# Grouped-query attention with two-bank score tiles, and the softmax's scale moved into the queries

## The chip, the core and the metric

The kernel runs on one core of one Trainium2 chip. A core has five engines that this text names: PE (TensorE, matrix multiplication, with its weight loads shown as PEld), DVE (VectorE), ACT (ScalarE), POOL (GpSimd) and SP (SyncE, which issues the DMAs here). Matmuls write to PSUM, which has 8 banks of 512 fp32 columns for each of 128 partitions; DVE and ACT read them from there. The metric is the device time of one execution in microseconds (us), lower is better.

## The reference

The program is a two-layer diffusion block on 512 image tokens and 256 context tokens with 1024 features, in fp32. Layer 0 has a feed-forward part, grouped-query attention and a second feed-forward part; layer 1 has differential attention in the attention's place. The change is in grouped-query attention alone: 16 query heads share 4 key and value heads of 64 columns. Cut to what matters:

```python
def sink_softmax(s):
    m = jnp.maximum(jnp.max(s, axis=-1, keepdims=True), sink)
    e = jnp.exp(s - m)
    return e / (jnp.sum(e, axis=-1, keepdims=True) + jnp.exp(sink - m))

# image queries, in blocks of 128: keys within 128 positions, and all context keys
s_loc = where(mask, einsum('bqkgd,bskd->bkgqs', qb, kb) * scale, NEG_INF)
s_ctx = einsum('bqkgd,bckd->bkgqc', qb, kc) * scale          # scale = 64 ** -0.5 = 0.125
p = sink_softmax(concatenate([s_loc, s_ctx], axis=-1))
out = einsum(p[..., :span], vb) + einsum(p[..., span:], vc)
# context queries attend to the context keys alone
```

## The kernel before

Activations lie transposed, features on partitions and the 768 tokens along the columns. To hold fp32 accuracy on a faster format, each operand is split into a high and a low part (`w_hi` and `w_lo`, `xh` and `xl`, `kh` and `kl`, `pth` and `ptl`), and a product is two or three matmuls. `weights` (L54 to L56) loads a weight block by DMA, ACT rounds it to the high part, POOL subtracts for the low part.

The function `gqa` is one stage of the program. Its PSUM is divided into pools: `pgqa` (1 bank, `half`) for the projections, `pgqa_t` (2 banks, `tr`) for transposes, `pgqa_v` (1 bank, `av`) for the weighted values and `pgqa_s` (4 banks, `s`) for scores. A tile of a pool is given out again when its last reader is done, in a ring.

The stage first projects one unit of keys, two of queries and one of values, through the score banks, in two halves of 384 tokens each (`project_halves`, L285; the second half has two more columns, which become the unit's bias, L289). `norm_halves` sums the squares of the input with a matmul of ones (L248) and computes the inverse root into `rstd` on ACT and DVE (`rsqrt`, L218 to L223); `scaled_halves` (L297) multiplies the projections by it. `rope` (L319 to L327) rotates queries and keys.

Then 24 steps follow, 4 key heads with 6 blocks of 128 queries each. A step computes the scores of four heads against 512, 640, 640, 512, 256 and 256 keys (`scores`). Each head has a bank of its own, or two where the keys are 640 (384 and 256 columns). Per bank: two matmuls (L437, L438), for image blocks one or two that add the mask (L441), a maximum on DVE (L443), the exponential on ACT with its sum (L450). For 640 keys the two maxima are merged (L446). L447 multiplies the maximum by -0.125 and takes the minimum with the negated sink. L453 to L457 make the reciprocal of the sum for four heads at once, and L460 (DVE) and L463 (POOL) scale the probabilities. `values` transposes them (L475), splits them (L478 on ACT, L479 on DVE), multiplies by the values (L480, L481) and puts the heads together (L485 to L494).

The loop issues the scores of step i+1, then a projection of a later unit or a part of the output projection (L520) as filling work, then the values of step i. The order on each engine is not written by hand: a scheduler fixes it at build time from its own estimate of durations, and each engine then works strictly in that order, waiting on semaphores.

## Time and profile before

| | |
|---|---|
| three runs | 2901.63, 2899.31, 2900.96 us, median 2900.96 |
| the profiled execution | 2902.44 us, of which its span 2900.6 us |
| mean granted TensorE clock | 0.982 |

The profile's stretches, in us busy of each engine:

| stretch (us) | what runs | PE | DVE | ACT | POOL | clock |
|---|---|---|---|---|---|---|
| 0 to 630 | start, feed-forward | 585.5 | 389.6 | 165.2 | 265.6 | 0.97 |
| 630 to 1000 | grouped-query attention | 336.7 | 284.3 | 213.6 | 169.4 | 0.96 |
| 1000 to 1900 | feed-forward, twice | 894.2 | 398.4 | 211.6 | 350.3 | 1.00 |
| 1900 to 2400 | differential attention | 476.3 | 298.6 | 208.1 | 257.1 | 0.99 |
| 2400 to 2900 | rest, feed-forward | 477.4 | 185.0 | 173.9 | 268.8 | 0.99 |

Matmuls are pipelined and their ends are modelled, so PE counts as busy also where it is not at its peak. An idle time is named by the instruction that waited and the one that ended the wait; where the wait had several conditions, by the last. In a group's row stand the line, the engine, the operation, output and inputs, shapes, the count, then the busy time in us and the mean duration in ns, then the idle time before them.

### The profile page before, as it was taken

The numbers are of one execution on the slowest core, as the hardware profiler recorded it, in microseconds if no ns is written. First come the engines' busy times: TensorE is split into PE (matmuls) and PEld (weight loads), VectorE is DVE, ScalarE is ACT, GpSimd is POOL, SyncE is SP. The second block draws the span as 40 slices with busy tenths as digits, with TensorE's granted clock in tenths as the row PEclk, the third lists the DMA queues.
The fourth block names the chain that finished last, engine by engine and source line by source line (L and its number), as shares of the span: only waits on it lengthen the run. The fifth ranks groups of instructions, "written<-read, shape, count | busy, mean of one in ns | idle before, by whom it ended". The sixth has DMA issues, their size and how long they took to land. (4 is left out here: it accounts for less than half of the span.)

```text
span 2900.6 us, 40961 instructions
## 1 busy us (share of the span) xinstructions
PE 2770.0 (95%) x16150; PEld 2593.4 (89%) x16150; DVE 1555.9 (54%) x2683; ACT 972.4 (34%) x1749; POOL 1311.2 (45%) x762
## 2 busy tenths in 40 slices
PE   5899999999989899999999999999989999999998
PEld 3899999989877799999998999999988887799998
DVE  7955555567887544444447333344467678522223
ACT  4322122145666421221224212221345555422223
POOL 4443343355443443333335433333465665555553
PEclk7999999999999999999999999999999999999999
DMA  6333333333242323233223232232232333233331
GB/s 240 121 112 108 125 105 118 124 115 100 82 144 81 99 78 112 76 106 117 74 90 106 75 118 84 91 120 88 85 98 74 90 89 114 83 92 100 102 105 44
DMA packets 113423, 296.38 MB, mean 102 GB/s; under 512 B 12880, under 2 KB 30928, under 8 KB 113232
## 3 DMA queue, kind: packets, MB, share of 16 engines
q1 hardware_dynamic: 112944, 293.66, 31.8%
q8 instruction: 128, 2.10, 0.3%
q14 instruction: 63, 0.52, 0.1%
q10 hardware_dynamic: 288, 0.10, 0.0%
HBM read 260.42 MB, written 15.20 MB: 95 GB/s over the span
## 5 line engine op out<-in xcount | busy, mean ns | idle before, releaser
L56 POOL TENSOR_TENSOR w_lo<-w_raw,w_hi 128x1024 fp32r<-128x1024 f32 (+2 forms) x377 | 802.1, 2128 | 1072.1 <-ACT w_hi L55 1055.6
L266 PE MATMUL big<-xh,w_hi 128*128 128x384 f32 (+3 forms) x2816 | 696.6, 328 | 38.7 <-DVE xh L831 19.5
L55 ACT CAST w_hi<-w_raw 128x1024 fp32r<-128x1024 f32 (+2 forms) x377 | 337.4, 895 | 1132.6 <-PE big L70 394.1
L266 PE MATMUL big<-xl,w_hi 128*128 128x384 f32 (+3 forms) x2816 | 693.6, 327 | 8.3 <-DVE xl L832 5.0
L266 PE MATMUL big<-xh,w_lo 128*128 128x384 f32 (+3 forms) x2816 | 693.6, 328 | 2.3 <-POOL w_lo L56 2.3
L266 PEld LDWEIGHTS big<-xh,w_hi 128*128 128x128 f32 x2816 | 502.5, 191 | 47.2 <-DVE xh L831 22.3
L266 PEld LDWEIGHTS big<-xl,w_hi 128*128 128x128 f32 x2816 | 500.3, 191 | 10.5 <-DVE xl L832 6.3
L266 PEld LDWEIGHTS big<-xh,w_lo 128*128 128x128 f32 x2816 | 497.8, 190 | 3.8 <-POOL w_lo L56 3.3
L131 DVE SCALAR_TENSOR_TENSOR ada_junk<-w_raw,s_bc 128x1024 f32<-128x1024 f32 x224 | 342.4, 1546 | 291.6 <-DMA w_raw<-ada_w 290.4
L271 DVE COPY bias<-big 128x2 f32<-128x2 f32 x176 | 27.7, 157 | 621.1 <-PE big L266 620.9
L68 PE MATMUL big<-hh,w_hi 128*128 128x512 f32 (+1 forms) x1200 | 327.6, 344 | 0.0
L70 PE MATMUL big<-hl,w_hi 128*128 128x512 f32 (+1 forms) x1200 | 327.3, 344 | 0.0
L72 PE MATMUL big<-hh,w_lo 128*128 128x512 f32 (+1 forms) x1200 | 326.8, 344 | 0.0
L311 DVE SCALAR_TENSOR_TENSOR hT<-big,mod,hT 128x512 f32<-128x512 f32 (+1 forms) x288 | 167.6, 618 | 176.7 <-PE big L72 176.4
L70 PEld LDWEIGHTS big<-hl,w_hi 128*128 128x128 f32 x1200 | 226.1, 188 | 29.5
L72 PEld LDWEIGHTS big<-hh,w_lo 128*128 128x128 f32 x1200 | 225.0, 188 | 28.6
L68 PEld LDWEIGHTS big<-hh,w_hi 128*128 128x128 f32 x1200 | 224.9, 188 | 27.2
L966 POOL TENSOR_TENSOR hl<-tb,hh 128x768 fp32r<-128x768 f32 (+1 forms) x88 | 152.3, 1730 | 183.2 <-ACT hh L965 181.9
L961 DVE SCALAR_TENSOR_TENSOR tb<-tb,bias,ta 128x512 f32<-128x512 f32 (+1 forms) x154 | 176.1, 1177 | 8.7 <-DVE tb L304 0.5
L285 PE MATMUL half<-xh,w_hi 128*128 128x384 f32 (+3 forms) x464 | 155.5, 335 | 20.6 <-DVE ta L297 18.8
L965 ACT CAST hh<-tb 128x768 fp32r<-128x768 f32 (+1 forms) x88 | 68.7, 781 | 276.5 <-DVE tb L961 276.5
L285 PE MATMUL half<-xl,w_hi 128*128 128x384 f32 (+3 forms) x464 | 153.8, 331 | 0.0
(215 smaller groups left out, 3677.6 us busy)
## 6 DMA issues: line engine op xcount, KB each, us to landing
w_raw<-ffn_gu SPq DMA_DIRECT2D x176, 512.0 KB, 3.3
w_raw<-ada_w SPq DMA_DIRECT2D x128, 512.0 KB, 3.3
w_raw<-ffn_d SPq DMA_DIRECT2D x96, 256.0 KB, 2.7
w_raw<-ffn_d SPq DMA_DIRECT2D x64, 320.0 KB, 2.9
w_raw<-diff_in SPq DMA_DIRECT2D x24, 512.0 KB, 3.2
ada_raw<-ada_w SPq DMA_DIRECT2D x16, 512.0 KB, 7.2
w_raw<-gqa_in SPq DMA_DIRECT2D x12, 512.0 KB, 3.5
og<-god SPq DMA_DIRECT2D x6, 768.0 KB, 6.5
```

The lines of the kernel that those rows point to most:

```text
L55: nc.scalar.copy(out=hi[:, :cols], in_=raw[:, :cols])
L56: nc.gpsimd.tensor_tensor(out=lo[:, :cols], in0=raw[:, :cols], in1=hi[:, :cols].bitcast(F32), op=ALU.subtract)
L68: nc.tensor.matmul(o, wh, xh, start=(k == 0), stop=False)
L70: nc.tensor.matmul(o, wh, xl, start=False, stop=False)
L72: nc.tensor.matmul(o, wl, xh, start=False, stop=(k == n - 1))
L131: getattr(nc, engines[s]).scalar_tensor_tensor(out=junk, in0=raw, scalar=1.0, in1=self.sbc[:, s], op0=ALU.mult, op1=ALU.mult, accum_out=se ...
L266: mm(ps[:, c, :e - s], w[:, k], x[:, k, s:e], start=first, stop=last)
L285: mm(ps[:, :e - s], w_[:, k], x[:, k, s:e], start=(k == 0 and i == 0), stop=(k == ND - 1 and i == 2))
L311: self.nc.vector.scalar_tensor_tensor(out=h, in0=o, scalar=self.mv(l, s, c, d), in1=h, op0=ALU.mult, op1=ALU.add)
L961: nc.vector.scalar_tensor_tensor(out=u[:, tk], in0=u[:, tk], scalar=bu[:, s:s + 1], in1=g[:, tk], op0=ALU.add, op1=ALU.mult)
L965: nc.scalar.copy(out=hh[:, toks], in_=u[:, toks])
L966: nc.gpsimd.tensor_tensor(out=hl[:, toks], in0=u[:, toks], in1=hh[:, toks].bitcast(F32), op=ALU.subtract)
```

## The change

The score pool becomes two tiles of two banks each. A tile holds one head of 640 keys (320 columns in each bank), two heads of 512 (a bank each) or four of 256 (two in a bank). One reduce gives the negated maxima of all heads of a tile, one instruction takes the minimum with the negated sinks (a tensor_scalar for one head, a tensor_tensor for two or four), and one exponential covers a head, across both banks where it has 640 keys. The factor 0.125 no longer stands in L447 and L450: the queries and their bias are multiplied by it as they are scaled by `rstd`. The early projections and the norm, which share the score pool, use a two-bank tile each; they go through `project_k`, which takes both halves of an input block before the next block. `project_halves` and `scaled_halves` gain an argument that other callers leave out.

```diff
+    def project_banks(self, src, pool, xonly=False, scale=None):
+        ps = pool.tile([P, 2, 512], F32, name="s")
+        self.project_k([(self.weights(src), ps)], range(ND), xonly)
+        n = 256 if xonly else 384
+        return (ps[:, 0], ps[:, 1]), self.bias_of(ps[:, 1, n:n + 2], scale)
+
+    def bias_of(self, ps, scale=None):
+        bias = self.sp.tile([P, 2], F32, name="bias")
+        if scale:
+            self.nc.vector.tensor_scalar(out=bias, in0=ps, scalar1=scale, scalar2=None, op0=ALU.mult)
+        else:
+            self.nc.vector.tensor_copy(out=bias, in_=ps)
+        return bias
+
+    def norm_banks(self, pool):
+        ps = pool.tile([P, 2, 512], F32, name="s")
+        for i in range(2):
+            tk = slice(i * 384, i * 384 + 384)
+            self.nc.tensor.matmul(ps[:, i, :384], self.ones, self.acc[:, tk], start=True, stop=True)
+        for i in range(2):
+            tk = slice(i * 384, i * 384 + 384)
+            self.rsqrt(self.rstd[:, tk], ps[:, i, :384], 1.0 / D)
...
-            self.nc.vector.tensor_tensor(out=u[:, tk], in0=ps[i][:, :n], in1=self.rstd[:, tk], op=ALU.mult)
+            if scale:
+                self.nc.vector.scalar_tensor_tensor(out=u[:, tk], in0=ps[i][:, :n], scalar=scale, in1=self.rstd[:, tk],
+                                                    op0=ALU.mult, op1=ALU.mult)
...
-        pss = self.ps("pgqa_s", 4)
+        pss = self.ps("pgqa_s", 2)
...
-        early = self.project_halves(a["gqa_in"][8], pool=pss, tag="s")
-        self.norm_halves(pss)
+        early = self.project_banks(a["gqa_in"][8], pss)
+        self.norm_banks(pss)
...
-            u, bias = project(i, pool)
+            u, bias = project(i, pool, scale=0.125)
...
-                for c, (b, n) in enumerate(((0, 384), (384, 256)) if w == 640 else ((0, w),)):
-                    s = pss.tile([P, 512], F32, name="s")[:, :n]
...
-                    nc.vector.tensor_reduce(out=st[:, 4 * c + h:4 * c + h + 1], in_=s, op=ALU.max, axis=AX.X)
-                    ss.append((c, b, n, s))
-                if len(ss) == 2:
-                    nc.vector.tensor_tensor(out=mx[:, h:h + 1], in0=mx[:, h:h + 1], in1=st[:, 4 + h:5 + h], op=ALU.max)
-                nc.vector.tensor_scalar(out=nm[:, h:h + 1], in0=mx[:, h:h + 1], scalar1=-0.125,
-                                        scalar2=nsink[:, hh:hh + 1], op0=ALU.mult, op1=ALU.min)
-                for c, b, n, s in ss:
-                    nc.scalar.activation(out=p[:, b:b + n], in_=s, func=AF.Exp, bias=nm[:, h:h + 1], scale=0.125,
-                                         accum_out=st[:, 8 + 4 * c + h:9 + 4 * c + h])
+            per = 1024 // w
+            n = w // 2 if per == 1 else w
+            for h0 in range(0, 4, per):
+                two = pss.tile([P, 2, 512], F32, name="s")
+                if per == 4:
+                    two = two.rearrange("p c (h n) -> p (c h) n", h=2)
...
+                nc.vector.tensor_reduce(out=mx[:, hs], in_=two[:, :, :n], op=ALU.max,
+                                        axis=AX.XY if per == 1 else AX.X, negate=True)
+                sink = nsink[:, 4 * g + h0:4 * g + h0 + per]
+                if per == 1:
+                    nc.vector.tensor_scalar(out=nm[:, hs], in0=mx[:, hs], scalar1=sink, scalar2=None, op0=ALU.min)
+                else:
+                    nc.vector.tensor_tensor(out=nm[:, hs], in0=mx[:, hs], in1=sink, op=ALU.min)
+                for i in range(per):
...
+                    nc.scalar.activation(out=dst, in_=s, func=AF.Exp, bias=nm[:, h:h + 1], accum_out=sm[:, h:h + 1])
...
-            for c in range(len(ss)):
-                nc.vector.tensor_tensor(out=e, in0=e, in1=st[:, 8 + 4 * c:12 + 4 * c], op=ALU.add)
+            nc.vector.tensor_tensor(out=e, in0=e, in1=sm, op=ALU.add)
```

The scheduler's order changes within this stage alone. PE has as many matmuls as before, DVE 152 instructions fewer, ACT 32. In the changed kernel line numbers are higher: L297 is L323, L443 is L476, L447 is L480 or L482, L453 to L460 are L490 to L496, L479 is L515, and the score matmuls L437, L438, L441 are L471, L472, L474.

DVE at the beginning of the stage, from the bias of the first keys to their scaling, before (`s` the score banks, `tb` and `ta` temporaries):

```order
L289 COPY bias<-s 128x2
L219 TENSOR_SCALAR tb<-s 128x384 x2
L221 TENSOR_TENSOR tb<-tb,ta 128x384 x2
L222 SCALAR_TENSOR_TENSOR tb<-tb,ta 128x384 x2
L223 SCALAR_TENSOR_TENSOR rstd<-tb,ta 128x384 x2
L297 TENSOR_TENSOR ta<-s,rstd 128x384 x3
```

and in the changed kernel:

```order
L286 COPY bias<-s 128x2
L219 TENSOR_SCALAR tb<-s 128x384
L221 TENSOR_TENSOR tb<-tb,ta 128x384
L222 SCALAR_TENSOR_TENSOR tb<-tb,ta 128x384
L219 TENSOR_SCALAR tb<-s 128x384
L223 SCALAR_TENSOR_TENSOR rstd<-tb,ta 128x384
L221 TENSOR_TENSOR tb<-tb,ta 128x384
L323 TENSOR_TENSOR ta<-s,rstd 128x384
L222 SCALAR_TENSOR_TENSOR tb<-tb,ta 128x384
L223 SCALAR_TENSOR_TENSOR rstd<-tb,ta 128x384
L323 TENSOR_TENSOR ta<-s,rstd 128x384
```

The second L219, the last to read the norm's banks, has moved behind the first half's L221 and L222.

DVE in a step of 640 keys, from a reduce to the scaling of the first head (`st` the step's small columns, `p` the probabilities, `ptl` the low part of the transposed ones of the step before), before:

```order
L443 TENSOR_REDUCE st<-s 128x1
L479 TENSOR_TENSOR ptl<-tr,pth 128x512
L443 TENSOR_REDUCE st<-s 128x1 x3
L446 TENSOR_TENSOR st<-st 128x1
L479 TENSOR_TENSOR ptl<-tr,pth 128x512
L446 TENSOR_TENSOR st<-st 128x1
L447 TENSOR_SCALAR st<-st,nsink 128x1 x2
L453 TENSOR_TENSOR st<-st,sinks 128x4
L456 TENSOR_TENSOR st<-st 128x4 x2
L457 RECIPROCAL st<-st 128x4
L460 TENSOR_SCALAR p<-p,st 128x640
```

and in the changed kernel:

```order
L476 TENSOR_REDUCE st<-s 128x1 x2
L480 TENSOR_SCALAR st<-st,nsink 128x1 x2
L490 TENSOR_TENSOR st<-st,sinks 128x4
L515 TENSOR_TENSOR ptl<-tr,pth 128x512
L492 TENSOR_TENSOR st<-st 128x4
L493 RECIPROCAL st<-st 128x4
L515 TENSOR_TENSOR ptl<-tr,pth 128x512
L496 TENSOR_SCALAR p<-p,st 128x640
```

The merges L446 and the second L456 are gone, each reduce covers a whole head, and fewer instructions stand between two L479 (now L515).

PE where the first key head's second step of 512 keys begins, with the tiles' numbers (`s_5729` is one score tile, `kh` and `kl` the keys, `qs` a head's queries), before:

```order
L437 MATMUL s_5729<-kh_5108,qs_5189 128x512
L438 MATMUL s_5729<-kl_5109,qs_5189 128x512
L441 MATMUL s_5729<-mask_4976,identr_4977 128x128
L437 MATMUL s_5737<-kh_5108,qs_5190 128x512
L438 MATMUL s_5737<-kl_5109,qs_5190 128x512
L441 MATMUL s_5737<-mask_4976,identr_4977 128x128
L285 MATMUL half_6072<-xh_95,w_hi_6042 128x386
```

and in the changed kernel:

```order
L471 MATMUL s_5683<-kh_5106,qs_5186 128x512
L472 MATMUL s_5683<-kl_5107,qs_5186 128x512
L474 MATMUL s_5683<-mask_4976,identr_4977 128x128
L471 MATMUL s_5683<-kh_5106,qs_5187 128x512
L472 MATMUL s_5683<-kl_5107,qs_5187 128x512
L474 MATMUL s_5683<-mask_4976,identr_4977 128x128
L471 MATMUL s_5696<-kh_5106,qs_5261 128x512
L472 MATMUL s_5696<-kl_5107,qs_5261 128x512
L474 MATMUL s_5696<-mask_4976,identr_4977 128x128
L471 MATMUL s_5696<-kh_5106,qs_5262 128x512
L472 MATMUL s_5696<-kl_5107,qs_5262 128x512
L474 MATMUL s_5696<-mask_4976,identr_4977 128x128
```

Two heads now share a tile (`s_5683`, then `s_5696`), and all four heads stand together where filling work (`half`) stood between the second and the third.

More of the change, by code (lines that the diff above doesn't have):

```diff
@@ L287, in project_halves, with scaled_halves @@
         n = 256 if xonly else 384
[L288 to L292 removed]
+        return out, self.bias_of(out[1][:, n:n + 2], scale)
+    def scaled_halves(self, ps, tag, xonly=False, scale=None):
         u = self.tp.tile([P, T], F32, name=tag)
@@ new lines, in scores @@
+            n = w // 2 if per == 1 else w
+            for h0 in range(0, 4, per):
+                hs = slice(h0, h0 + per)
+                two = pss.tile([P, 2, 512], F32, name="s")
+                if per == 4:
+                    two = two.rearrange("p c (h n) -> p (c h) n", h=2)
+                for i in range(max(per, 2)):
+                    h = h0 + (0 if per == 1 else i)
+                    q = qs[h][:, qc]
+                    b = i * n if per == 1 else 0
+                    s = two[:, i, :n]
@@ L435, in scores @@
                     ks = slice(c0 + b, c0 + b + n)
[L436 removed]
+                    ms = [(side, off - b) for side, off in masks if b <= off < b + n]
                     nc.tensor.matmul(s, q, kh[:, ks], start=True, stop=False)
[L438 to L442 removed]
@@ L449, in scores @@
-                for c, b, n, s in ss:
-                    nc.scalar.activation(out=p[:, b:b + n], in_=s, func=AF.Exp, bias=nm[:, h:h + 1], scale=0.125,
-                                         accum_out=st[:, 8 + 4 * c + h:9 + 4 * c + h])
-                out.append(p)
+                    nc.tensor.matmul(s, q, kl[:, ks], start=False, stop=not ms)
+                    for side, off in ms:
+                        nc.tensor.matmul(s[:, off:off + P], identr, mask[:, side * P:side * P + P], start=False,
+                                         stop=True)
@@ L453, in scores @@
+                for i in range(per):
+                    h = h0 + i
+                    p = rpp.tile([P, 640], F32, name="p")
+                    dst, s = ((p.rearrange("p (c n) -> p c n", c=2), two[:, :, :n]) if per == 1 else
+                              (p[:, :n], two[:, i, :n]))
+                    nc.scalar.activation(out=dst, in_=s, func=AF.Exp, bias=nm[:, h:h + 1], accum_out=sm[:, h:h + 1])
+                    out.append(p)
             nc.vector.tensor_tensor(out=e, in0=nm, in1=sinks[:, 4 * g:4 * g + 4], op=ALU.add)
```

31 lines of the change are left out of this document (10 added, 21 removed).

## The prediction

> **What bounds the kernel now.** I read the busy line and the slices of the page first, then the stretch of the attention stage by engine, then what PE waited for there, then the costs of the lines that the change touches.
>
> ```profile
> PE 2770.0 (95%) x16150; PEld 2593.4 (89%) x16150; DVE 1555.9 (54%) x2683; ACT 972.4 (34%) x1749; POOL 1311.2 (45%) x762
> ```
>
> PE sets the time: it is busy 95% of the span. The attention stage is the stretch from 650 to 940 us (columns: PE, PEld, DVE, ACT and POOL busy, granted clock, DMA share, GB/s):
>
> ```profile
> 650.00:940.00 290.00, 268.75 (x1566) 238.39 (x1565) 230.53 (x585) 181.41 (x488) 134.15 (x129) 0.98 0.33 100
> ```
>
> There PE is idle for 290 - 268.75 = 21.3 us. DVE is busy 79% of that stretch against 54% of the span, so here it is the engine that PE is most likely to wait for. No step of the change touches the other stages. What this change can win is bounded by those 21 us and by what the clock loses there.
>
> ```profile
> PE av L480 <- DVE o L488: 4.9, 4, 1.6
> PE tr L475 <- DVE st L447: 3.3, 2, 2.4
> PE s L437 <- ACT p L450: 2.1, 3, 1.7
> PE av L480 <- ACT qs L372: 1.9, 1, 1.9
> PE half L285 <- DVE st L447: 1.8, 1, 1.8
> PE av L481 <- DVE ptl L479: 1.6, 6, 0.4
> PE av L480 <- ACT pth L478: 1.2, 2, 0.6
> PE half L285 <- DVE ta L297: 0.8, 1, 0.8
> PE tr L475 <- DVE st L446: 0.7, 1, 0.7
> ```
>
> These are PE's waits in that stretch (total, times, longest). DVE ended 4.9 + 3.3 + 1.8 + 1.6 + 0.8 + 0.7 = 13.1 us, ACT 2.1 + 1.9 + 1.2 = 5.2 us, together 18.3.
>
> **What the change takes from DVE.**
>
> ```profile
> L443 DVE TENSOR_REDUCE st<-s 128x1 f32<-128x256 f32 x64 | 25.9, 414 | 2.2 <-PE s L441 1.0 <-PE s L438 0.9
> L443 DVE TENSOR_REDUCE st<-s 128x1 f32<-128x512 f32 x32 | 21.6, 684 | 7.7 <-PE s L441 7.5
> L447 DVE TENSOR_SCALAR st<-st,nsink 128x1 f32<-128x1 f32 x96 | 18.4, 205 | 0.5
> L443 DVE TENSOR_REDUCE st<-s 128x1 f32<-128x384 f32 x32 | 17.5, 548 | 1.8 <-PE s L441 1.6
> L446 DVE TENSOR_TENSOR st<-st 128x1 f32<-128x1 f32 x32 | 15.4, 488 | 0.3
> ...
> L453 DVE TENSOR_TENSOR st<-st,sinks 128x4 f32<-128x4 f32 x24 | 8.5, 354 | 0.2
> L456 DVE TENSOR_TENSOR st<-st 128x4 f32<-128x4 f32 x32 | 7.5, 235 | 3.9 <-ACT st L454 3.5
> ```
>
> - Maxima: 128 reduces, 25.9 + 21.6 + 17.5 = 65.0 us, become 24 over 1024 columns (16 of two heads, 8 of four) and 32 over 640. From 256 to 512 columns a reduce grows by 270 ns, so 1024 gives 684 + 540 = 1224 ns and 640 gives 684 + 135 = 819. That is 29.4 + 26.2 = 55.6 us, 9.4 less. No row shows a reduce across two banks. If it costs as much as two (1368 and 962 ns) the sum is 63.6, only 1.4 less. I take 9.4, since the three shapes lie on one line.
> - The merge of two maxima (L446) goes: 15.4 us.
> - The subtracted maximum (L447): 96 become 32 of the same kind (6.6 us) and 24 tensor_tensor of two or four heads. The nearest row is L453, with the same kind of operands, 354 ns: 8.5 us. So 15.1 instead of 18.4, 3.3 less. By L446's 488 ns nothing is won here; by its shortest, 142 ns (shown next), 8.4.
> - One addition of the sums a step less in the 640-wide steps: 8 x 235 ns = 1.9 us.
>
> The sum is 30 us of DVE's 230.5, with ends at 19 and 35. The queries' bias and scaling keep their count (a copy becomes a multiply, a multiply takes a scalar as well). Beside the scaling's 1.47 us for three stands a scalar_tensor_tensor of the same width at 1.01 us for two (both quoted with the stage's start below): nothing.
>
> L446 is dear for so little work because of what it meets:
>
> ```profile
> L446 DVE TENSOR_TENSOR st<-st x32: 142/160/1972, 677.0 to 904.8; 128x1 f32<-128x1 f32 x32
> L447 DVE TENSOR_SCALAR st<-st,nsink x96: 182/204/216, 669.0 to 928.5; 128x1 f32<-128x1 f32 x96
> ...
> 780.26 2.38 POOL L56 TENSOR_TENSOR w_lo<-w_raw,w_hi 128x1024 fp32r<-128x1024 f32 x1 [0.29 <-ACT w_hi L55]
> 780.69 1.97 DVE L446 TENSOR_TENSOR st<-st 128x1 f32<-128x1 f32 x1
> 783.25 0.54 DVE L297 TENSOR_TENSOR ta<-half,rstd 128x384 f32<-128x384 f32 x1
> 783.93 0.41 PE L285 MATMUL half<-xh,w_hi 128*128 128x384 f32 x1 [1.78 <-DVE st L447]
> ```
>
> Shortest, median and longest: a one-column tensor_tensor takes 160 ns, or up to 1972, while the tensor_scalar never leaves 182 to 216. At 780.69 it starts inside POOL's L56 and ends as that ends (782.6). L297, which frees the projection's bank, stands behind it, and PE waits 1.78 us. With L446 this wait goes. POOL's instructions stay, though, and L453, L456 and the 24 new tensor_tensor can still meet them: 88 such small instructions become 72.
>
> [...]
>
> **What it takes from ACT.**
>
> ```profile
> L450 ACT ACTIVATE p<-s,st 128x256 f32<-128x256 f32 x64 | 30.2, 475 | 3.4 <-PE tr L475 3.4
> L450 ACT ACTIVATION_READ_ACCUMULATOR p<-s,st 128x1 f32 x128 | 26.0, 204 | 0.0
> L450 ACT ACTIVATE p<-s,st 128x512 f32<-128x512 f32 x32 | 21.8, 688 | 11.6 <-PE tr L475 7.5 <-DVE st L447 3.4 <-PE s L438 0.7
> L450 ACT ACTIVATE p<-s,st 128x384 f32<-128x384 f32 x32 | 18.7, 583 | 16.1 <-DVE st L447 12.3 <-PE half L285 3.7
> ```
>
> 96.7 us now. Afterwards 32 of 256, 32 of 512 and 32 of 640 columns, the last at 688 + 106 = 795 ns on the line of the others, with 96 reads of the accumulator: 15.2 + 22.0 + 25.4 + 19.6 = 82.2, 14.5 less. If the 640 costs as much as its two parts (1058 ns), 6.1 less.
>
> PE's own work stays: as many matmuls, 320 + 320 columns for 384 + 256.
>
> **How much of it reaches PE.** There are 24 steps in the stretch; each loses 30 / 24 = 1.3 us on DVE and 0.6 on ACT, while PE waits 0.55 us a step for DVE and 0.2 for ACT. So the ends are 0 (the removed work was not in front of a wait) and 18.3 us (all waits gone). I take half, 9.2: of the waits of 1.8 us and longer, the one at 781.7 holds a removed instruction, while the 2.4 us one, at 802, is started by an L456 held by POOL's L373, which stays:
>
> ```profile
> 801.42 1.82 POOL L373 TENSOR_TENSOR ta<-ta,qs 128x768 f32<-128x768 f32 x1 [1.93 <-ACT qs L372]
> 801.45 1.80 DVE L456 TENSOR_TENSOR st<-st 128x4 f32<-128x4 f32 x1
> ```
>
> **What the start of the stage pays.**
>
> ```profile
> 635.46 0.62 PE L285 MATMUL s<-xh,w_hi 128*128 128x384 f32 x2 [0.48 <-ACT xh L193]
> 641.69 0.45 PE L285 MATMUL s<-xh,w_hi 128*128 128x384 f32 x1 [0.75 <-DVE tb L219]
> ...
> 641.08 1.07 DVE L219 TENSOR_SCALAR tb<-s 128x384 f32<-128x384 f32 x2 [1.23 <-ACT ta L218]
> 642.07 1.88 DVE L221 TENSOR_TENSOR tb<-tb,ta 128x384 f32<-128x384 f32 x2
> 643.88 1.01 DVE L222 SCALAR_TENSOR_TENSOR tb<-tb,ta 128x384 f32<-128x384 f32 x2
> 645.76 1.47 DVE L297 TENSOR_TENSOR ta<-s,rstd 128x384 f32<-128x384 f32 x3
> ```
>
> The score pool's tiles go round in a ring, and the first query projection gets the banks of the norm. Now its first half starts when the first L219 has read one bank. Afterwards it needs both banks, and the second L219 stands behind an L221 and an L222: 642.07 + 0.94 + 0.50 + 0.54 = 644.1 instead of 641.7, so PE loses 2.4 us with nothing else placed there. The half-by-half wait for the last input block at 635.46 (0.5 us) goes, since both halves of the earlier blocks come first. Net 1.9 us lost; ends 0 and 2.4.
>
> **The clock.**
>
> ```profile
> 800.00:810.00 10.00, 7.41 (x31) 5.51 (x30) 7.34 (x18) 5.62 (x18) 4.11 (x5) 0.70 0.33 85
> 820.00:830.00 10.00, 7.67 (x40) 5.86 (x38) 8.88 (x24) 8.91 (x25) 7.10 (x6) 0.90 0.96 315
> 830.00:840.00 10.00, 8.46 (x55) 7.46 (x54) 8.65 (x25) 7.05 (x22) 5.14 (x5) 0.93 0.87 312
> 920.00:930.00 10.00, 8.45 (x40) 6.44 (x41) 7.58 (x24) 6.12 (x18) 3.42 (x5) 0.83 0.27 79
> ```
>
> The granted clock dips where PE pauses: 3.0 + 1.0 + 0.7 + 1.7 = 6.4 us of clock lost. Ends 0 and 6.4; with half of the waits gone I take half of the largest dip, 1.5. [...]
>
> **Sum.** -9.2 + 1.9 - 1.5 = -8.8 us. The profiled execution took 2902.4 us (its span 2900.6 and 1.8 around it); the median of the three shown is 2901.0, 1.5 below it. So 2893.6 for such an execution, 2892.1 for the median.
>
> **Rivals.**
> - *Everything goes.* All 18.3 us of waits and the whole 6.4 of clock: -18.3 - 6.4 + 1.9 = -23; I put it at 2880. For it: more work is removed a step than PE waits. Against: the waits held by POOL's long instructions, and ACT's L372, stay.
> - *Absorbed.* The new tensor_tensor meet POOL as L446 did (24 x 0.488 = 11.7 us) and the waits that remain (L488, L479) move on to the chain of transpose, cast and subtraction, which is unchanged. Then -4 to +4, about 2900. For it: L488 and L479, 6.5 of the 13.1 us, wait on work that the change leaves alone.
> - *Slower: the two-bank release.* Place: the 512-wide steps, L437 waiting for its bank. Now a bank is free after its own reduce, 205 ns and exp: 0.68 + 0.2 + 0.69 = 1.6 us after its matmuls. Afterwards both wait for the joint reduce and two exps: 1.22 + 0.35 + 2 x 0.69 = 3.0, so 1.4 us later, on 16 tiles: 22 us if nothing covers it. It decides from 7 exposed tiles on (7 x 1.4 = 9.8, more than my 9.2); with 12 the sum is -8.8 + 16.8 = +8, 2909. Against: PE now waits for ACT's exps only 3 times; for the 640-wide tiles the release is no later, 0.82 + 0.2 + 0.8 = 1.8 against 0.55 + 0.41 + 0.49 + 0.2 + 0.58 = 2.2.
> - *It does not do what it says* is ruled out: the order has 152 DVE and 32 ACT instructions fewer.
>
> **Chances.** Forecast (-14 to -4) 0.50, everything 0.12, absorbed 0.27, two-bank release 0.11. A difference under 0.2% (5.8 us) is about what a measurement of this kernel cannot tell from none. Of the forecast about 0.46 lies beyond it, with 0.12 from the first rival and 0.02 from the edge of the second: faster 0.60; slower 0.10; same 0.30. Range: 2880 (the first rival, and the best ends of DVE's sum) to 2904 (the dear ends of the reduce and of the start, with half of the release's price), leaving out some 0.15.
>
> **What would show it.** DVE's busy time in the stage about 200 us, the 1024-wide reduce near 1.2 us and the 640-wide near 0.8; exps of 640 near 0.8. PE's waits ended by DVE near 7 us. At the start, PE's wait on L219 near 3 us instead of 0.75. For the two-bank rival: more time of score matmuls waiting for exps. I am wrong if PE's idle time in the stage stays near 21 us though DVE's work falls.

## The result, and the profile after

| | median (us) | runs | against before |
|---|---|---|---|
| before, on the same chip | 2900.53 | 2899.31 to 2901.63 | |
| changed kernel | 2917.55 | 2914.47 to 2921.01 | 1.0057, interval 1.0044 to 1.0069 |

The change costs 17 us, 0.57%, where 8.8 us less was predicted. The profiled execution of the changed kernel took 2921.0 us (span 2919.1).

In the attention stage the operations became as cheap as the prediction put them. Groups of the changed kernel with shapes kept apart (count, busy us, mean ns), then one line's shortest, median and longest instruction:

```profile
L476 DVE TENSOR_REDUCE st<-s 128x1 f32<-128x640 f32 x32 | 26.1, 820 | 12.1 <-PE s L474 11.8
L488 ACT ACTIVATE p<-s,st 128x640 f32<-128x640 f32 x32 | 25.4, 796 | 15.0 <-DVE st L480 13.9 <-DVE st L493 0.9
L476 DVE TENSOR_REDUCE st<-s 128x2 f32<-128x1024 f32 x16 | 19.4, 1214 | 3.8 <-PE s L474 3.8
...
L482 DVE TENSOR_TENSOR st<-st,nsink x24: 144/154/1030, 674.2 to 929.5; 128x2 f32<-128x2 f32 x16, 128x4 f32<-128x4 f32 x8
```

A reduce over two banks lies on the line of the narrower ones: 820 and 1214 ns where 819 and 1224 were estimated, and the exp of 640 columns takes 796 ns where 795 were. The new tensor_tensor takes 154 ns in the middle and up to 1030: 6 of the 24 take 357 ns or more, each until an instruction of POOL ends.

The stretch from 650 to 940 us (PE, PEld, DVE, ACT, POOL busy, clock, DMA share, GB/s), and PE's waits in it (total, times, longest):

```profile
650.00:940.00 290.00, 268.82 (x1570) 240.92 (x1568) 203.02 (x423) 169.98 (x412) 130.66 (x124) 0.96 0.33 99
...
PE av L517 <- DVE ptl L515: 6.3, 9, 1.9
PE half L556 <- DMA og<-god: 4.0, 3, 2.4
PE av L516 <- DVE o L524: 3.2, 4, 2.3
PE av L516 <- ACT pth L514: 2.5, 3, 1.3
PE half L309 <- DVE ta L320: 2.3, 2, 1.4
PE s L471 <- ACT p L488: 2.0, 3, 1.3
```

DVE went from 230.5 to 203.0 us and ACT from 181.4 to 170.0. (The changed kernel reaches its first scores 4.5 us later, so this window holds a little less of the stage; over the same PE work, shown below for e1, DVE goes from 221 to 200.) PE is idle 290 - 268.82 = 21.2 us, as before. The waits for the removed work (`st`, L446 and L447, together 5.8 us) are gone, and as much has come up behind the subtraction `ptl` (1.6 before, 6.3 now), the cast `pth` (1.2, now 2.5) and the loads of `og`. The waits of score matmuls for exps stand where they stood, 2.0 us in three.

Two other places lost time. One is the start of the stage. Its window in the kernel before:

```profile
640.00:650.00 10.00, 9.25 (x50) 8.51 (x50) 8.38 (x15) 3.62 (x7) 3.67 (x2) 1.00 0.16 52
```

and in the changed kernel:

```profile
640.00:650.00 10.00, 6.56 (x27) 5.68 (x26) 7.13 (x14) 4.21 (x7) 3.63 (x2) 0.83 0.16 54
```

The entry of the changed kernel's timeline that accounts for it (start, length, instruction, the wait ahead of it and its releaser):

```profile
644.77 1.01 PE L266 MATMUL s<-xh,w_hi 128*128 128x384 f32 x2 [3.44 <-DVE tb L219]
```

PE waits 3.44 us for VectorE's work at the old bank before the next projection's matmuls, and the granted clock drops to 0.83. The other place is a feed-forward stage, which no edit touches. A window of 200 us in the kernel before:

```profile
1200.00:1400.00 200.00, 200.00 (x1140) 190.71 (x1139) 94.41 (x142) 40.31 (x52) 75.56 (x38) 1.00 0.31 100
```

and in the changed kernel:

```profile
1200.00:1400.00 200.00, 200.00 (x1134) 189.98 (x1133) 91.46 (x138) 40.73 (x53) 76.25 (x38) 1.00 0.31 99
```

PE is busy throughout at full clock in both, with six matmuls fewer afterwards. Setting each matmul of the one trace beside the same of the other shows the difference growing evenly through these stages, from 10.7 us at 1015 us to 14.9 at 1974.

### The profile page after: what moved, and what is told of

It is laid out like the page before. It is cut to its first block, busy times and chain, and to the rows that moved or that the text cites. A ratio compares the mean times of both kernels' runs of the same rounds, so it can differ in the third digit from the quotient of the medians.

```text
span 2919.1 us, 40715 instructions
## 1 busy us (share of the span) xinstructions
PE 2782.6 (95%) x16150; PEld 2599.7 (89%) x16150; DVE 1543.0 (53%) x2531; ACT 967.1 (33%) x1685; POOL 1309.7 (45%) x762
## 5 line engine op out<-in xcount | busy, mean ns | idle before, releaser
L131 DVE SCALAR_TENSOR_TENSOR ada_junk<-w_raw,s_bc 128x1024 f32<-128x1024 f32 x224 | 348.8, 1574 | 292.1 <-DMA w_raw<-ada_w 290.7
```

The source lines that it names most:

```text
L131: getattr(nc, engines[s]).scalar_tensor_tensor(out=junk, in0=raw, scalar=1.0, in1=self.sbc[:, s], op0=ALU.mult, op1=ALU.mult, accum_out=se ...
```

## Experiments

Times are medians; a ratio is that to the kernel before on the same chip, whose medians lay between 2901.5 and 2904.1 us. Of single profiles a difference of 3 us in the stage is no evidence: one and the same order took 264.6 and 268.1 us for its 24 steps in two of the runs below (e14 and e18, which differ in addresses alone), at clocks of 0.99 and 0.97.

### The stages that the change does not touch: where the tiles lie

**e1.** In the changed kernel:

```diff
-            st = self.sp.tile([P, 16], F32, name="st")
+            st = self.sp.tile([P, 24], F32, name="st")
```

> The changed kernel with the small statistics tile st kept at 24 columns instead of 16 (8 columns are never touched), so that every SBUF tile behind it lies where it lay before the change; all engines' orders are those of the changed kernel. In the two profiles, stages that the change does not touch also run slower after it: between 1200 and 1400 us PE is busy throughout at full clock in both, with 1140 matmuls before and 1134 after, and the later of two 512-column matmuls of the feed-forward (input hh) starts 235 ns after the earlier instead of 229. Theory A, addresses: the smaller st moves hh by 128 bytes and that is what makes these matmuls slower; then this kernel has 229 to 231 ns there again, about 1140 matmuls in 1200 to 1400 us, and takes 7 to 10 us less than the changed one, 2907 to 2910 us. Theory B, the chip or the moment of that one profile: then 235 or 229 ns, but the time stays at the changed kernel's 2917 within its scatter of 3 us. The rest (9 us) is the attention stage and stays.

**e2.** In the kernel before:

```diff
-            st = self.sp.tile([P, 24], F32, name="st")
+            st = self.sp.tile([P, 32], F32, name="st")
```

> The kernel before with st grown from 24 to 32 columns (never touched): the SBUF tiles behind it move by 128 bytes the other way, the orders are the same on all engines. Theory A (addresses decide the pace of the 512-column matmuls, and the shift by half of 256 bytes is what counts): 235 ns, and 7 to 10 us slower than before, 2908 to 2911. If only the direction or a coarser grid counts: the pace stays at 229 to 231 ns and the time at 2900.5. Theory B: no change, 2900.5 within 2.

**e8.** In the kernel before:

```diff
         self.sp = self.sb("smalls", 4)
+        self.sp.tile([P, 48], F32, name="gap", bufs=1)
```

> The kernel before with 192 unused bytes behind the small tiles; no order changes. Sorted by where in 256 bytes their input starts, the 512-column matmuls of the runs so far start one after the other every 229 to 231 ns (start at 192, before), 234 to 235 ns (start at 64, after the change and in the second run), 226 to 227 ns (start at 128, the output of the differential attention in the second run). Here hh starts at 128. If the start within 256 bytes sets the pace: 226 to 227 ns, 2016 matmuls of hh and hl by 3 ns, 6 us less than before, about 2895.5. If the pace at 128 was particular to that other input: 229 to 235 ns and 2901 to 2909.

The same stretch in e1, the changed kernel with the old addresses:

```profile
1200.00:1400.00 200.00, 200.00 (x1140) 190.67 (x1139) 90.40 (x140) 41.44 (x54) 76.69 (x38) 1.00 0.32 101
```

in e2, the kernel before with moved ones:

```profile
1200.00:1400.00 200.00, 200.00 (x1134) 190.03 (x1133) 90.47 (x138) 39.56 (x52) 74.43 (x37) 1.00 0.32 101
```

and in e8, with others again:

```profile
1200.00:1400.00 200.00, 200.00 (x1143) 190.61 (x1142) 93.83 (x140) 40.07 (x52) 77.47 (x39) 1.00 0.31 101
```

1140 matmuls where `hh` starts as it did before, 1134 where it starts as in the changed kernel, and 1143 in e8:

| kernel | `hh` starts at byte, modulo 256 | 512 columns (ns) | 256 columns (ns) | time (us) | ratio |
|---|---|---|---|---|---|
| before | 63424, 192 | 229.8 | 119.2 | | |
| changed | 63296, 64 | 234.9 | 118.4 | 2917.55 | 1.0057 |
| e1 | 63424, 192 | 229.8 | 119.1 | 2909.51 | 1.0025 (1.0015 to 1.0034) |
| e2 | 63552, 64 | 234.7 | 118.6 | 2907.24 | 1.0021 (1.0012 to 1.0030) |
| e8 | 63616, 128 | 231.7 | 115.1 | 2898.99 | 0.9993 (0.9984 to 1.0002) |

The two columns in ns are means from start to start of the feed-forward's second matmuls in this stretch, 216 of each width, worked out from the trace. Theory A, that it is the addresses, holds from both sides, with no order changed: `st` has four buffers, each 32 bytes smaller, so everything behind it moves by 128 bytes (the weights' tiles lie ahead of it and stay), and a wide and a narrow one of these matmuls together take 353.3 instead of 348.9 ns. The trace has 2016 of 512 columns and 1776 of 256. Their times from start to start, set one by one against the same matmul of the other trace and added up, make 7.4 us between the changed kernel and e1 (8.8 on the wide ones, 1.4 back on the narrow ones) and 7.6 between e2 and the kernel before. Measured were 8.0 by the medians (2917.55 to 2909.51) or 9.3 by the ratios (1.0057 to 1.0025), and 5.7 in the other direction. Between e1 and the kernel before the difference no longer grows in these stages: 7.4 us at 1015 us, 7.3 at 1974. In e8 the expected 226 ns did not come; the wide matmuls got slower and the narrow ones faster, 346.7 ns together. By the same sum it should gain 3.6 us, and gained 2.5, an interval that includes none; 6 were expected.

### The scale, and the start of the stage

**e3.** The scale alone, in the kernel before: `project_halves` and `scaled_halves` with their new argument, and

```diff
-            u, bias = project(i, pool)
+            u, bias = project(i, pool, scale=0.125)
...
-                nc.vector.tensor_scalar(out=nm[:, h:h + 1], in0=mx[:, h:h + 1], scalar1=-0.125,
+                nc.vector.tensor_scalar(out=nm[:, h:h + 1], in0=mx[:, h:h + 1], scalar1=-1.0,
...
-                    nc.scalar.activation(out=p[:, b:b + n], in_=s, func=AF.Exp, bias=nm[:, h:h + 1], scale=0.125,
+                    nc.scalar.activation(out=p[:, b:b + n], in_=s, func=AF.Exp, bias=nm[:, h:h + 1],
```

> The kernel before with one part of the change alone: the factor 0.125 goes into the queries and their bias, the score tiles and the start of the stage stay. The order is the same on every engine. My prediction puts this part at nothing: 2900.5 within 2 us. If the multiply with a scalar on the queries' scaling costs, DVE gets slower by 8 units x 2 instructions, at most 16 x 0.1 = 1.6 us, and a little of it reaches PE.

2902.67 us, ratio 1.0005 (0.9996 to 1.0014): nothing, as predicted.

**e4.** In e1:

```diff
-        self.norm_banks(pss)
+        self.norm_banks(ptr)
...
-        ps = pool.tile([P, 2, 512], F32, name="s")
...
+            ps = pool.tile([P, 512], F32, name="tr")[:, :384]
```

> The kernel of the first run of this group (changed kernel, old addresses), with the norm's two sums of squares written to the two transpose banks, which are free at that point, instead of a two-bank score tile: the first query projection then has a score tile that nobody holds. The scheduler makes another order for the whole stage. By my account of the stage's start the 3.4 us wait of the first query projection for the second L219 goes, and with it 1 to 2 us of lower clock: 3 to 5 us less than the first run of this group if the rest of the stage costs the same. Rival, the order: the scheduler's new order of the 24 steps matters more than this wait, and the time may then lie up to 8 us on either side, with PE's idle time between 650 and 940 us other than the first run's by more than 4 us.

2907.96 us, ratio 1.0019 (1.0010 to 1.0028). The wait is gone: the window of 640 to 650 us has PE busy for 10.00 us at full clock, and the first scores start 4.0 us earlier than in e1 (666.4 instead of 670.4). Of this 1.5 us arrive at the end, where 3 to 5 were expected, and the intervals of e1 and e4 overlap. The rival named for it, another order further on, asked for an idle time of PE between 650 and 940 us that differs by more than 4 us; it is 20.9 us in e1 and 23.8 in e4. So the rival's mark is not reached, and where the rest went stays open.

### The end of the stage

The last head group's output goes through memory: `god` is written, `og` is read back in three pieces, the image columns' two first and the context columns last. PE at this place in the kernel before (start, length, instruction, wait and releaser):

```profile
950.71 0.40 PE L520 MATMUL half<-og,w_lo 128*128 128x512 f32 x1
953.41 0.97 PE L520 MATMUL half<-og,w_hi 128*128 128x256 f32 x4 [2.31 <-DMA og<-god]
```

and in e1:

```profile
951.69 0.52 PE L556 MATMUL half<-og,w_lo 128*128 128x256 f32 x2
958.26 1.01 PE L556 MATMUL half<-og,w_hi 128*128 128x256 f32 x2 [6.06 <-DMA og<-god]
```

Before, nine matmuls of the image columns (512 wide) stand ahead of the first one that needs the last piece; in the changed kernel's order that one comes first, and ready work waits behind it.

**e6** in e4, and **e7** in the kernel before:

```diff
+                for cs in ((1,), (0,)) if part == (2, 3) else ((0, 1),):
                   for d, i, (wh, wl), outs in todo:
...
-                            for ps, (s, tk) in zip(outs, cuts):
+                            for ps, (s, tk) in [(outs[x], cuts[x]) for x in cs]:
...
-                    if part[-1] == 3:
+                    if part[-1] == 3 and 0 in cs:
```

> The fourth run's kernel (norm in the transpose banks) with the first matmuls of the second output projection in another order: all 24 of the image columns of the last head group, whose piece of the attention's output lands first, then the 24 of the context columns, whose piece lands last. The rest of the order stays. In the fourth run PE waits 5.1 us for that last piece with the ready matmuls queued behind it (48 matmuls stand ahead of the wait; before the change 57 and a wait of 2.3 us). Expected: 72 matmuls ahead of the wait, the wait at 0 to 1 us, 4 to 5 us less than the fourth run: about 2903.5. If the order at this place does not matter, 2908.

> The same edit in the kernel before, where 57 matmuls stand ahead of the wait and it lasts 2.3 us: the wait goes, 2 us less than before, about 2899.5. That is the part of the difference at the end of the stage that the order of these matmuls can explain, taken from the other side.

e6: 2895.79 us, 0.9979 (0.9970 to 0.9988). e7: 2895.83 us, 0.9977 (0.9967 to 0.9987). PE's waits from the last `av` to 1000 us in e4:

```profile
PE big L266 <- DVE hT L335: 9.2, 1, 9.2
PE half L554 <- DMA og<-god: 5.1, 1, 5.1
```

and in e6:

```profile
PE big L266 <- DVE hT L335: 4.6, 1, 4.6
PE half L555 <- POOL w_lo L56: 0.8, 1, 0.8
```

Ten microseconds of this place in e4:

```profile
950.00:960.00 10.00, 7.38 (x34) 6.45 (x35) 3.29 (x6) 3.26 (x6) 0.21 (x1) 0.83 0.18 52
```

and in e6:

```profile
950.00:960.00 10.00, 9.15 (x55) 7.67 (x54) 9.81 (x14) 7.62 (x13) 4.66 (x3) 1.00 0.29 93
```

The edit was expected to give 4 to 5 us in e4 and 2 in before, and gave about 12 and 6. The wait for `og` was only the first half: while PE waits, no output tile is finished, and DVE, which adds them to `hT` (3.29 us busy in these ten, 9.81 with the edit), starts later; the next stage's first matmul then waits for DVE (9.2 us, now 4.6). The granted clock of these ten is 0.83 in e4 and 1.00 in e6. By the whole time the edit gains some 5 to 6 us more in the changed order than in the old one, a number uncertain by nearly as much. By the profiles, from the last `av` to the same matmul of the next stage near 1007 us, it saves 9.7 us in e4 and 7.0 in the kernel before, 2.7 more. So some 3 to 6 us are what the order of these few matmuls cost the change.

### The 24 steps

The steps always hold the same 1470 PE instructions, up to the last `av`. The window over them in the kernel before:

```profile
666.70:940.40 273.70, 252.45 (x1473) 222.04 (x1472) 221.08 (x571) 175.79 (x480) 122.71 (x123) 0.98 0.31 96
```

in e1:

```profile
670.00:943.60 273.60, 251.23 (x1473) 222.15 (x1472) 200.18 (x419) 168.19 (x415) 121.06 (x123) 0.97 0.31 95
```

and PE's longest waits there in e1:

```profile
PE av L517 <- DVE ptl L515: 6.6, 9, 1.8
PE av L516 <- ACT pth L514: 4.6, 5, 1.9
PE av L516 <- DVE o L524: 4.0, 3, 2.3
```

21 us less on DVE and 8 on ACT, and the steps are as long as they were. Is DVE's work not in front of PE's waits at all?

**e5** in e1, and **e11** in e7:

```diff
-                nc.vector.tensor_reduce(out=mx[:, hs], in_=two[:, :, :n], op=ALU.max,
+                nc.vector.tensor_reduce(out=mx[:, hs], in_=two[:, :, :32], op=ALU.max,
...
-                    nc.vector.tensor_reduce(out=st[:, 4 * c + h:4 * c + h + 1], in_=s, op=ALU.max, axis=AX.X)
+                    nc.vector.tensor_reduce(out=st[:, 4 * c + h:4 * c + h + 1], in_=s[:, :32], op=ALU.max, axis=AX.X)
```

> The first run's kernel (changed kernel, old addresses) with each maximum taken over the first 32 columns of each part of the tile instead of all (the maxima are then others than the reference's; exp and sums follow them). A reduce should fall from 0.82 and 1.21 us to some 0.2 to 0.3, so DVE does about 40 us less in the 24 steps: near 160 us instead of 200 between the first score matmul and the last av. Theory C, DVE's work is not in front of PE's waits: the change's own saving gave PE nothing in the steps (from the first score to the last av 273.3 us before and 273.2 after, PE idle 21.3 and 22.4), so this larger one gives nothing either: 273 us within 3, PE idle 20 to 25, the waits again on the chain transpose, cast, subtraction (ptl, pth, o), total 2909.5 within 3. Rival D, DVE is still the engine that the steps wait for and only an unlucky order hid the gain: the steps get shorter by 6 us or more, total below 2904.

> The seventh run's kernel (before the change, with the new hand-over; 2895.8) with each maximum taken over the first 32 columns of its bank (maxima other than the reference's). DVE does 128 reduces at 0.2 instead of 0.41, 0.55 and 0.68 us, about 40 us less. That asks of the old tiles what the prediction asked: what is DVE work in the steps worth there. Theory D: 0.3 for each us, 10 us and more: 2884 to 2888. The prediction's half of the waits for DVE's scores (st: 6.5 us) and the rest at their old size: 3 to 5 us, 2891 to 2893. If DVE's work is not in front of PE's waits: 2895.8 within 2.

**e10** in e6:

```diff
                     nc.vector.tensor_tensor(out=nm[:, hs], in0=mx[:, hs], in1=sink, op=ALU.min)
+                nc.vector.tensor_reduce(out=st[:, 16 + h0:16 + h0 + per], in_=two[:, :, :n], op=ALU.max,
+                                        axis=AX.XY if per == 1 else AX.X)
```

> The sixth run's kernel with each joint maximum computed a second time, behind the minimum, into columns of st that nothing reads: about 55 us more DVE work in the steps (204 to 258 of 274 us busy). Theory D: 31 us less DVE work gave 9 us in the fifth run, 0.3 for each, so 10 to 16 us more: 2906 to 2912. Theory G: the second reduce stands in front of ptl as well, so more time too, and more than half of it in PE's waits for ptl. If DVE's work has slack in the steps: less than 5 us more.

The window over the steps in e5, to be set beside e1's above:

```profile
668.30:932.80 264.50, 246.34 (x1473) 219.10 (x1472) 169.99 (x419) 167.46 (x415) 122.59 (x123) 0.99 0.32 99
```

in e7, and behind it e11, the same with shortened maxima:

```profile
667.30:938.40 271.10, 249.06 (x1472) 219.53 (x1471) 221.51 (x571) 176.02 (x480) 122.85 (x123) 0.99 0.31 97
```

```profile
665.40:930.00 264.60, 248.87 (x1473) 221.57 (x1472) 193.17 (x571) 175.27 (x480) 122.87 (x123) 0.97 0.32 99
```

in e6, and behind it e10, the same with every maximum twice:

```profile
663.90:938.30 274.40, 252.34 (x1471) 222.04 (x1471) 203.90 (x419) 168.25 (x415) 123.80 (x123) 0.97 0.31 95
```

```profile
663.90:960.40 296.50, 256.65 (x1473) 223.69 (x1472) 243.42 (x475) 168.90 (x415) 123.89 (x123) 0.97 0.29 88
```

e5: 2900.92 us, 0.9996 (0.9987 to 1.0004), 8.6 less than e1. e11: 2887.87, 0.9952 (0.9939 to 0.9966), 8.0 less than e7. e10: 2916.05, 1.0046 (1.0033 to 1.0059), 20 more than e6. Theory C, that the steps do not wait for DVE's work, does not hold. From e1 to e5, 30 us less on DVE shorten the steps by 9.1; from e7 to e11, 28 us by 6.5; from e6 to e10, 40 us more lengthen them by 22. That is 0.23 to 0.30 for a microsecond removed, and 0.56 for one added (theory D had expected 10 to 16 us for e10). By the medians of the whole time (8.6, 8.0 and 20 us) it is 0.28 twice, and 0.5. At the lower price the change's 21 us should have given 5 to 6. Something took them back.

These prices are not pure. Each of the three edits also makes the scheduler choose another order: about a thousand of PE's 16150 places hold another matmul than in the kernel it is set against, and what an order alone is worth is shown below. For DVE's work itself speaks that all three go the way of the work, and that PE's waits for `ptl` fall from 6.6 us in e1 (shown above) to 1.5 in e5 and rise from 5.5 in e6 to 9.5 in e10 (e5, e6 and e10 in this order):

```profile
PE av L517 <- DVE ptl L515: 1.5, 5, 0.6
```

```profile
PE av L515 <- DVE ptl L513: 5.5, 6, 1.8
```

```profile
PE av L517 <- DVE ptl L515: 9.5, 12, 2.2
```

The maxima also stand ahead of the exp, so that a shorter one shortens a chain as well; what a microsecond of the other removed instructions is worth was not tried.

**e9** in e6, and **e13**, the same in e1: one maximum and one minimum a head.

```diff
+                for i in range(per):
+                    h = h0 + i
+                    nc.vector.tensor_reduce(out=mx[:, h:h + 1], in_=two[:, :, :n] if per == 1 else two[:, i, :n],
+                                            op=ALU.max, axis=AX.XY if per == 1 else AX.X, negate=True)
+                    nc.vector.tensor_scalar(out=nm[:, h:h + 1], in0=mx[:, h:h + 1],
+                                            scalar1=nsink[:, 4 * g + h:4 * g + h + 1], scalar2=None, op0=ALU.min)
```

> The sixth run's kernel (two-bank tiles, old addresses, norm in the transpose banks, new hand-over; 2895.8) with one reduce and one minimum for each head of a two- or four-head tile, as before the change, instead of one of each for the tile. DVE works some 10 us more in the steps: 64 reduces at 0.41 or 0.68 us and 64 minima at 0.2, 48 us, for 24 at 1.21 and 24 at 0.26 to 0.35, 37 us. Between the first score matmul and the last av the sixth run takes 273.8 us, the seventh (before, with the same hand-over) 270.5. Theory G, grain: a joint reduce of 1.2 us makes the first exp of a tile and the subtraction (ptl) that stands behind it on DVE wait longer than the shorter reduces did, and that eats what the saved work gives; then the steps get 3 to 6 us shorter and PE waits 2 to 3 us for ptl instead of 5.5; total 2890 to 2893. Theory D, DVE's busy time counts whatever its grain: the steps get 2 to 4 us longer, 2898 to 2900. Neither (the order alone decides): within 2 us of 2895.8.

> The first run's kernel (the change with the old addresses, its own start and end; 2909.5) with one reduce and one minimum for each head. Theory G (grain): 4 to 6 us less, as in the ninth run, 2903.5 to 2905.5; the steps from first score to last av at 268 to 270 us instead of 273. If the ninth run's gain was the luck of one order: anything from 2905 to 2914, its sign open. Theory D alone (10 us more DVE work): 2911 to 2913.

e9: 2890.63 us, 0.9962 (0.9949 to 0.9974). e13: 2905.31, 1.0016 (1.0008 to 1.0025). Both are faster than the joint maximum, by 5.2 and 4.2 us of the medians or 4.9 and 2.6 of the ratios (in both cases the intervals overlap), with more work on DVE, as theory G asked, by which a joint reduce holds DVE in too long a piece. A place in e1's timeline, with other instructions left out, shows how a joint reduce would cost:

```profile
809.45 1.21 DVE L476 TENSOR_REDUCE st<-s 128x2 f32<-128x1024 f32 x1
810.57 0.40 DVE L523 TENSOR_TENSOR o<-av,o 64x256 f32<-64x256 f32 x1
810.99 0.43 DVE L524 TENSOR_TENSOR o<-av,o 64x256 f32<-64x256 f32 x1
811.56 0.47 PE L516 MATMUL av<-pth,vs 128*128 128x512 f32 x1 [2.27 <-DVE o L524]
```

DVE is held for 1.21 us ahead of the two additions that free the `av` bank. But the total of the waits for `ptl`, which the theory put at 2 to 3 us, stayed at 5.5 in e9; and in e10, where it asked for more than half of the added time there, these waits grew by 4.0 of 22 us. So it was tried whether the order alone does as much.

**e14** in e6, **e15** the same in e9, **e17** the like in e7 (`for h in (3, 2, 1, 0)`):

```diff
-            for h0 in range(0, 4, per):
+            out = [None] * 4
+            for h0 in range(4 - per, -1, -per):
...
-                    out.append(p)
+                    out[h] = p
```

> The sixth run's kernel (joint maxima, 2895.8) with the tiles of a step issued from the last heads to the first: the same instructions, another order. It measures what an order alone does: within 2 us of 2895.8 (steps 273.8 within 2), and run 9's 5.2 us are more than that; or 4 us and more away, and then run 9 alone shows nothing of the grain.

> The ninth run's kernel (a maximum per head, 2890.6) with the tiles of a step issued from the last heads to the first. With theory G it stays below the fourteenth run by 3 us or more, near 2890.6 within 2. With luck of the order, the two reversed kernels may stand the other way round.

> The seventh run's kernel (score tiles before the change, new hand-over; 2895.8) with the heads of a step issued from the last to the first: the same instructions in another order. If the order alone decides on both sides: 4 us or more away from 2895.8, the sign open. If the old tiles, a head to a bank, are less sensitive to it: within 2 us; then the two-bank tiles win by 10 us in their better order (e14, 2885.9), and the change's saving of DVE work was real and hidden by its first order.

The window over the steps in e14:

```profile
664.60:929.20 264.60, 247.57 (x1473) 218.67 (x1472) 200.70 (x419) 169.11 (x415) 123.34 (x123) 0.99 0.32 99
```

in e9, and behind it e15, the same with the heads reversed:

```profile
664.80:934.90 270.10, 251.30 (x1473) 220.93 (x1472) 209.50 (x499) 168.48 (x416) 123.29 (x123) 0.97 0.31 97
```

```profile
663.00:934.50 271.50, 253.81 (x1473) 223.57 (x1472) 210.56 (x499) 168.74 (x415) 123.48 (x123) 0.96 0.31 97
```

| score tiles | heads 0 to 3 | heads 3 to 0 |
|---|---|---|
| before (e7, e17) | 0.9977 (0.9967 to 0.9987) | 0.9974 (0.9964 to 0.9984) |
| two banks, joint maximum (e6, e14) | 0.9979 (0.9970 to 0.9988) | 0.9951 (0.9938 to 0.9963) |
| two banks, a maximum per head (e9, e15) | 0.9962 (0.9949 to 0.9974) | 0.9959 (0.9947 to 0.9971) |

Theory G falls as a general statement: with the heads reversed the joint maximum is no slower (0.9951 against 0.9959), and the reversal alone, with the same instructions, is worth 0.28%, 8 us, to the joint tiles. The same pair at other addresses (e12 and e18 below) says 0.26%. The old tiles don't feel it (0.9977 and 0.9974). So in the reversed order, with start and end mended, the two-bank tiles are 0.23% ahead of the old ones (e14 against e17), 6.7 us, near the 6 that 21 us of DVE's work are worth at 0.28. The steps of e14 have 17.0 us of idle PE where e6 has 22.1, and a mean clock of 0.99 instead of 0.97, by an estimate 5 us more (0.02 of 264.6); e18, in e14's order, has 17.8 us and again 0.97, so that only the idle time clearly goes with the order. What in the order of e6 makes the difference is not settled.

### Versions that are faster than both

The line of e8 in e6 (**e12**), in e9 (**e16**) and in e14 (**e18**):

> The sixth run's kernel with the 192 unused bytes of the eighth (input hh of the 512-column matmuls starts at 128 of 256 bytes); the order is the sixth run's. The eighth run took 2.5 us less than before. If the address decides independently of the rest: 2.5 us less than 2895.8, 2893.3, and below the kernel before by 0.2 to 0.3%.

> The ninth run's kernel with the 192 unused bytes of the eighth and twelfth runs, which gave 2.5 and 4.9 us: 2886 to 2888, the fastest of the kernels that compute the reference's softmax with its own maxima, 0.5% below the kernel before.

> The fourteenth run's kernel (joint maxima, heads reversed, norm in the transpose banks, new hand-over; 2885.9) with the 192 unused bytes, which gave 2.5, 4.9 and 4.6 us in the eighth, twelfth and sixteenth run: 2881 to 2883.

e12: 2890.87 us, 0.9962 (0.9950 to 0.9975). e16: 2886.07, 0.9951 (0.9939 to 0.9964). e18: 2885.52, 0.9936 (0.9923 to 0.9948), on a chip where the kernel before took 2904.08; that is the fastest, 18.6 us below it, though 2881 to 2883 were expected. In e12 and e18 a wide and a narrow one of the feed-forward's matmuls take 346.7 ns as in e8, and e16 has, like e8, 1143 matmuls from 1200 to 1400 us. Against the same kernels without that line the ratio falls by 0.0017 (e12 beside e6), 0.0011 (e16 beside e9) and 0.0015 (e18 beside e14), which is 3 to 5 us. The matmuls over `hh` and `hl`, added up as above, make 4.4, 2.8 and 4.1 us of it; the intervals of each two overlap.

## Why the prediction was wrong, point by point

- **"No step of the change touches the other stages": false, and the largest loss.** The prediction put this term at nothing. The tile of statistics shrank by a third and moved every tile behind it by 128 bytes. The feed-forward's matmuls over `hh` and `hl` became 1.3% slower where a wide and a narrow one alternate: 8.0 us (e1), seen from the other side as 5.7 (e2), and 7.4 and 7.6 added up in the traces. Nothing in the diff but the tile's width tells of it, and the argument from the stage's 21 us of idle could not hold it.
- **"How much of it reaches PE", half of 18.3 us: this step failed.** The cost of every operation was right. The sum of 30 us, though, adds up durations, and these overlap (at 783.71 us in the kernel before three L447, 205 ns each on average, take 0.44 us together): over the same PE work DVE's busy time fell by 21 us, from 221 to 200, and the 203 us in the window from 650 to 940 us met the forecast of 200 partly because the stage came later. PE's idle time stayed at 21 us, which the prediction named as the sign of its own failure. Removed waits were counted as won: those for `st` went, and waits for `ptl`, `pth` and `og` took their place. That is the mechanism of the rival "absorbed", without the end that it gave. DVE's work does count in these steps, at 0.23 to 0.30 for a microsecond removed (e5, e11, with the order's part in it); by that price 21 us are worth 5 to 6, less than the 9.2 of the forecast. And an order alone is worth as much: nothing arrives in the order of the change, while the heads reversed gain about 8 us of the whole time (e14 against e6). Which instructions of that order stand in the way stays open.
- **The end of the stage was not looked at.** The view from which the 18.3 us of waits were taken also has a row for `og` (0.8 us), which the prediction's list leaves out with three shorter ones (1.1 us together). A transfer that was nearly covered before (2.3 us) was exposed (6.1 us in e1) since nine ready matmuls came to stand behind it, and DVE's additions started late. The difference between e6's gain and e7's puts it at 3 to 6 us; in the profiles, e1 is 3.2 us behind the kernel before at the last `av` and 7.4 us at 1007 us, 4.2 us for the end.
- **The start: the right mechanism, a little too small.** 1.9 us were predicted, with a wait near 3 us on L219; the wait is 3.44 us, and e1's PE, 0.5 us behind the kernel before as the stage begins, is 3.2 us behind after the wait: 2.7 us. That is above the upper end of 2.4; the clock fell to 0.83 there, which the term did not count.
- **The clock: wrong in sign.** 1.5 us were to be won; the mean from 650 to 940 us went from 0.98 to 0.96 (0.97 in e1). These are one profile each, and e14 and e18 show 0.99 and 0.97 for one order, so it may be scatter; the last section has the stretches of half clock in two traces.
- **The two-bank release: not exposed.** Score matmuls wait 2.0 us for exps in three waits, 2.1 before. That rival had the right sign and the wrong mechanism.
- **New tensor_tensor and POOL: cheaper than taken.** 154 ns in the middle, 291 on average, 1030 at most, where 354 were taken. 6 of the 24 take 357 ns or more and end within 0.02 us of an instruction of POOL: that of 1030 ns starts at 722.95 us, inside POOL's L349 (722.67, 1.29 us long), and ends with it.
- **The scale in the queries: right,** nothing (e3).
- **A slip of reading, without weight:** the wait put at 781.7 us runs from 782.15 to 783.93; 781.7 is where the matmul ahead of it starts.

In sum, of 17 us some 7 to 9 are addresses; e1's remaining 0.25%, 7.3 us, are in its profile 2.7 at the start, 0 in the steps and 4.2 at the end, each with the uncertainty of a single profile.

## What to carry to other kernels

When a change makes a tile smaller, look where the tiles behind it come to lie (here 128 bytes from where they lay), and compare the pace of matmuls in a stage that the diff does not touch; a stretch where PE is busy throughout makes the count of matmuls a measure of it (here 1140 and 1134 in 200 us). Where a scheduler fixes the order, price removed work by what it is worth to the engine that waits (here 0.23 to 0.30, the order's part included), expect the new order to add or take as much, and read at the stage's end which ready instructions stand behind a transfer. Issuing the same instructions from another end is a cheap way to learn how much of a result is order.

## What the runs showed of the hardware that was not expected

- The feed-forward's matmuls over 512 and over 256 columns, from start to start between 1200 and 1400 us, at full clock and with the same instructions around them, took 229.8 and 119.2 ns in the kernel before and 229.8 and 119.1 in e1, where their moving input (`hh`, `hl`) starts at 192 within 256 bytes. They took 234.9 and 118.4 in the changed kernel and 234.7 and 118.6 in e2, both at 64 though their `hh` lies 256 bytes apart, and 231.7 and 115.1 in e8, at 128. In these 200 us PE did 1140, 1134 and 1143 matmuls. No other starts were tried for them. Whether it is the moving input alone, or its place against the weights that load meanwhile, no run separates.
- The maximum over two banks in one instruction costs what the line through 256, 384 and 512 columns in one bank gives (1214 ns for 1024, where the line gives 1224).
- The same order of the same instructions differs by 3.5 us in the steps between e14 and e18 (264.6 and 268.1), with the mean clock at 0.99 and 0.97. The two also differ in where their tiles lie.
- In the clock records of the traces of the kernel before and of the changed kernel, the granted clock is half in 17 and in 19 stretches and full between them. The last of each is cut off by the end of the trace (9.63 and 10.51 us); the others are 3.41, 6.83, 10.24, 13.65 or 17.07 us long, one to five times 3.41, and the times between them are whole multiples of 3.41 us too. Counted from the start of the span, the clock changes at 1.95 us past such a multiple in the kernel before and at 2.57 in the changed one.
- Cut into pieces of that length, each of the two traces has 816 at full clock. In the kernel before, half clock follows 17 of them, in which PE was busy for 5 to 52%; it does not follow the other 799, in which PE was busy for 49% or more. In the changed kernel it follows 19, with 0 to 54%, and not the other 797, with 44% or more. In the kernel before the half clock from 804.09 us on follows such a piece: PE was busy in it for 1.44 of 3.42 us, 42%, and idle for its last 1.89 us, in the wait of 2.4 us near 802.
